# Hymba decode step: queries and keys transposed in float32, two heads at once, and split into high and low parts as they leave PSUM

## The chip, the cores and the metric

The kernel runs on one core of one Trainium2 chip. The metric is the device time of one execution in microseconds (us), as the median of several. One profiled execution of the same kernel gives the trace that the rows below come from.

## The reference

One layer of a hybrid decoder handles a prompt of 512 tokens and 8 sample tokens. After RMSNorm and one input projection, one half of the channels goes through a state-space scan and a gated unit, the other half through attention with 8 query heads of 64 values and 2 key heads. An output projection joins both. The part that matters here are the scores of two of the three attention branches of the prompt:

```python
q = rope(rms_norm(q.reshape(B, S, N_HEADS, HEAD_DIM), q_norm_w), pos)
ks = rms_norm(kv[:, :, 0::2], k_norm_w[:, None, :])
ks = rope(ks...)
...
s = jnp.einsum('bqgrd,bqgkjd->bqgrkj', q, kg, preferred_element_type=f32) * scale   # selected blocks
s = jnp.einsum('bqgrd,bwgd->bqgrw', q, kw, preferred_element_type=f32) * scale      # window
```

The scores are wanted in float32. TensorE multiplies float32r operands, so the kernel keeps each query and key as a high part (the value rounded to float32r) and a low part (the value minus the high part) and adds the products.

## The kernel before

The program is written with a tile framework. It allocates buffers from pools, adds all semaphore waits, and a scheduler with a timeline of its own decides in which order the instructions of an engine stand. `S` is ScalarE (ACT in the profile), `V` VectorE (DVE), `T` TensorE (PE), `G` GpSimd (POOL). A copy or a subtraction goes through the wrapper `PsumFirst`, so it has line L61 where it touches PSUM and L62 where it does not.

The span has three stages. From 0 to about 178 us the dense stage `dense` projects the inputs (lines L121 to L123 are the three matmuls of a product of split operands) and runs the scan. At the end the output projection `wo_mm` does the same kind of matmul. Between them `merge` interleaves two streams of steps:

- `prompt`: four `qk_tile(i)`, one for each 128 tokens, then `attention(i)`, then `glu`. `qk_tile` makes the transposed queries `QT` and keys `KT` (head dimension on the partitions, tokens along the row). For the queries of one head, partitions 0 to 63 of `QT` hold the high part and 64 to 127 the low part. For the keys of one group, `KT[g][0]` holds the high part twice, in both halves of the partitions, and `KT[g][1]` the low part twice. `attention(i)` starts with L1159 (queries against compressed keys) and L1216 (queries against keys). L1230 is the first transpose of its probabilities.
- `sample`: `compress_prompt` (L1097, L1109, then L1119, 64 small matmuls of `W1r` against `XP`, then the bias `hb` and a gelu in the tiles `gx` and `hidp`), then for each pair of sample tokens `gather_pair`: GpSimd fetches cache pages with an indirect DMA into `kvg` (L1319), VectorE copies them into `xr`, TensorE transposes them (L1328, L1338) into tiles `t`, and L1362 multiplies. The first fetches reuse the buffers of `W1r`, so they wait until L1119 has read them.

`qk_tile` before the change works in this order for a tile. ScalarE rounds 512 query columns to float32r (`qs`), VectorE subtracts to get the low part, and both stand side by side for each head. The same is done for the keys (`ks`). Then TensorE transposes with the float32r identity `identr`: L995 four times for each group of four heads, L1002 four times for the keys of a group. That is 16 transposes for a tile, 64 in all. ScalarE copies each finished bank into `QT` or `KT` in two instructions of 128 by 256.

The finished transposes land in PSUM tiles of the tag `a`, which has three banks that `attention` and the matmuls of other stages share: `BANKS = dict(a=3, t=2, c=2, ph=1)`. A bank can be written again only when its readers are done.

Of the kernel before, what the change touches and what calls it, by code (L numbers as in the profile page):

```python
# [8 lines left out]
F32 = mybir.dt.float32  # L9
F32R = mybir.dt.float32r  # L10
# [3 lines left out]
ALU = mybir.AluOpType  # L14
# [22 lines left out]
def hymba_step_kernel(  # L37
# [9 lines left out]
    G, T = nc.gpsimd, nc.tensor  # L47
# [18 lines left out]
    V, S = PsumFirst(nc.vector), PsumFirst(nc.scalar)  # L66
# [7 lines left out]
    last = {}  # L74
# [8 lines left out]
    def pt_(name, cols=1024, dt=F32, parts=128):  # L83
        return big.tile([parts, cols], dt, tag="P", name=nm(name), bufs=NP)
# [7 lines left out]
    def st(shape, name, dt=F32, bufs=1, tag=None):  # L92
        n = nm(name)
        return sm.tile(shape, dt, tag=tag or n, name=n, bufs=bufs)
# [15 lines left out]
    def pb(use):  # L110
        tag = ROUTE[use]
        return psum.tile([128, 512], F32, tag=tag, name=nm(tag), bufs=BANKS[tag])
# [48 lines left out]
    ident = cst[:, C_ID:C_ID + 128]  # L161
# [35 lines left out]
    p = pb("tr")  # L197
# [129 lines left out]
    x = lambda j, b, k: lambda: x_split(j, b, k)  # L327
# [97 lines left out]
    identb = st([128, 128], "identb", BF16)  # L425
    with tc.issue_after(last["x"].ins):
        V.tensor_copy(identb, ident)
    identr = st([128, 128], "identr", F32R)
    with tc.issue_after(last["x"].ins):
        V.tensor_copy(identr, ident)  # L430
    causb = st([128, 128], "causb", BF16)
    with tc.issue_after(last["x"].ins):
        V.tensor_copy(causb, cst[:, C_CAUS:C_CAUS + 128])
# [10 lines left out]
    def rowset(i):  # L444
        if i < 4:
            return 128, kvt[i], qraw[i // 2][:, 512 * (i % 2):512 * (i % 2) + 512]
        return 8, kvs, qsr
# [53 lines left out]
    p = pb("ac")  # L501
# [123 lines left out]
    for src, ct_ in ((c_re, CTr), (c_im, CTi)):  # L625
        cn = k2("cn", 256).rearrange("p (q n) -> p q n", n=64)
        nc.sync.dma_start(cn, src[0].rearrange("(q g) c n -> (g c) q n", q=4))
        p = pb("ac")
# [18 lines left out]
    for a, src in enumerate((state_re, state_im)):  # L647
        n0 = k1("n0")
        nc.sync.dma_start(n0, src[0].rearrange("b (a c) n -> (b a) (c n)", c=2))
        p = pb("ac")  # L650
# [312 lines left out]
    p = pb("tr")  # L963
# [12 lines left out]
    QT = [[ht("QT", 1024, F32R) for _ in range(2)] for _ in range(2)]  # L976
# [2 lines left out]
    KTv = lambda g, a: KT[g][a].rearrange("p (k n) -> p k n", k=2)  # L979

    def qk_tile(i):
        _, kv_, q_ = rowset(i)
        qs = pt_("qs", 1024, F32R).rearrange("p (h a d) -> p h a d", a=2, d=64)
        qh = q_.rearrange("p (h d) -> p h d", d=64)
        S.copy(qs[:, :, 0, :], qh)
        V.tensor_tensor(qs[:, :, 1, :], qh, qs[:, :, 0, :].bitcast(F32), op=ALU.subtract)
        ks = pt_("ks", 1024, F32R).rearrange("p (k g a e d) -> p k g a e d", k=2, g=2, a=2, d=64)
        for kd in range(2):
            kz = kv_[:, 256 * kd + 256:256 * kd + 384].rearrange("p (g d) -> p g d", g=2).unsqueeze(2).to_broadcast([128, 2, 2, 64])
            S.copy(ks[:, kd, :, 0], kz)  # L990
            V.tensor_tensor(ks[:, kd, :, 1], kz, ks[:, kd, :, 0].bitcast(F32), op=ALU.subtract)
        for g in range(2):
            p = pb("qk")
            for r in range(4):
                T.transpose(p[:, 128 * r:128 * r + 128].bitcast(F32R), qs[:, 4 * g + r].rearrange("p a d -> p (a d)"), identr)  # L995
            for hf in range(2):
                S.copy(QT[g][hf].rearrange("p (h n) -> p h n", n=512)[:, :, 128 * i:128 * i + 128],
                       p[:, 256 * hf:256 * hf + 256].rearrange("p (h n) -> p h n", n=128))
            p = pb("qk")
            for kd in range(2):  # L1000
                for a in range(2):
                    T.transpose(p[:, 256 * a + 128 * kd:256 * a + 128 * kd + 128].bitcast(F32R),  # L1002
                                ks[:, kd, g, a].rearrange("p e d -> p (e d)"), identr)
            for a in range(2):
                S.copy(KTv(g, a)[:, :, 128 * i:128 * i + 128],
                              p[:, 256 * a:256 * a + 256].rearrange("p (k n) -> p k n", n=128))
            yield 1


# [737 lines left out]
```

## Time and profile before

| what | value |
|---|---|
| median of 3 executions | 468.6 us (466.94 to 468.63) |
| the profiled execution, its own time | 465.36 us |
| its span in the profile | 463.5 us |
| granted TensorE clock, mean | 0.996 |

The time of an execution is the span and what lies around it, 1.9 us here. The profiled execution is 3.2 us below the median. How to read the rows: a row of a timeline has the start within the span, the duration of the row, and in brackets the idle time of its engine ahead of it and what ended that time. A matmul row's duration contains a pipeline of about a quarter of a microsecond, so the cost of one in a run is read from the distance of starts or from the chain, which counts each stretch of time once.

### The profile page before, as it was taken

The numbers are of one execution on the slowest core, as the hardware profiler recorded it, in microseconds if no ns is written. First come the engines' busy times: TensorE is split into PE (matmuls) and PEld (weight loads), VectorE is DVE, ScalarE is ACT, GpSimd is POOL, SyncE is SP. The second block draws the span as 40 slices with busy tenths as digits, with TensorE's granted clock in tenths as the row PEclk, the third lists the DMA queues.
The fourth block names the chain that finished last, engine by engine and source line by source line (L and its number), as shares of the span: only waits on it lengthen the run. The fifth ranks groups of instructions, "written<-read, shape, count | busy, mean of one in ns | idle before, by whom it ended". The sixth has DMA issues, their size and how long they took to land.

```text
span 463.5 us, 10940 instructions
## 1 busy us (share of the span) xinstructions
PE 449.1 (97%) x4258; PEld 382.8 (83%) x4258; DVE 348.4 (75%) x940; ACT 240.9 (52%) x585; POOL 94.7 (20%) x104
## 2 busy tenths in 40 slices
PE   8999999999999998699999999999999899999997
PEld 4989999899999998698677776767667689799886
DVE  6878999998998999385767857787658678683332
ACT  5913664756414319575765668565665646342100
POOL 3100000056433000552342224321323010000000
PEclk9999999999999999999999999999999999999999
DMA  8877533614617433566153443346354994411211
GB/s 290 251 224 174 82 72 109 187 34 90 144 50 217 137 75 75 189 184 182 45 173 100 140 180 101 128 133 232 95 175 144 229 233 144 124 58 58 69 47 48
DMA packets 75602, 62.83 MB, mean 136 GB/s; under 512 B 29230, under 2 KB 69024, under 8 KB 75424
## 3 DMA queue, kind: packets, MB, share of 16 engines
q1 hardware_dynamic: 66176, 36.74, 28.9%
q0 software_dynamic: 4816, 17.03, 11.4%
q10 hardware_dynamic: 4560, 8.39, 5.9%
q8 instruction: 33, 0.54, 0.5%
q14 instruction: 17, 0.14, 0.1%
HBM read 55.63 MB, written 10.70 MB: 143 GB/s over the span
## 4 chain that ended last, share of the span: by engine, by line
PE 71%; DVE 14%; DMA 8%; POOL 3%; issue 2%; ACT 2%; SPq 0%; DVEq 0%; POOLq 0%; ACTq 0%
PE a L121 11%; PE a L122 11%; PE a L123 10%; PE ph L1362 8%; DMA kvg<-in_cache_kv_dram,idx 4%; PE a L1216 3%; PE a L1252 3%; PE t L1243 3%; POOL rsq L168 3%; PE c L1535 3%; PE t L1338 2%; DVE ga L62 2%; PE t L1328 2%; PE ph L473 1%; DMA x<-in_x_prompt_dram 1%
## 5 line engine op out<-in xcount | busy, mean ns | idle before, releaser
L121 PE MATMUL a<-hTh,whi 128*128 128x256 f32 (+1 forms) x192 | 54.6, 285 | 0.5 <-DVE sg L61 0.5
L122 PE MATMUL a<-hTh,wlo 128*128 128x256 f32 (+1 forms) x192 | 54.9, 287 | 0.0
L123 PE MATMUL a<-hTl,whi 128*128 128x256 f32 (+1 forms) x192 | 53.4, 284 | 0.0
L168 POOL TENSOR_TENSOR rsq<-rsq,mhalf 128x6 f32<-128x6 f32 (+3 forms) x10 | 28.7, 2871 | 101.2 <-DVE rsq L62 101.2
L1319 POOL DMA_INDIRECT kvg<-in_cache_kv_dram,idx x32 | 32.6, 1020 | 67.9 <-DVE ks L62 37.7
L122 PE MATMUL a<-whi,hTl 128*128 128x256 f32 (+1 forms) x160 | 45.7, 287 | 0.0
L121 PE MATMUL a<-whi,hTh 128*128 128x256 f32 (+1 forms) x160 | 45.2, 287 | 0.0
L123 PE MATMUL a<-wlo,hTh 128*128 128x256 f32 (+1 forms) x160 | 45.2, 284 | 0.0
L1362 PE MATMUL ph<-XT,W1h 128*128 128x256 f32 x256 | 44.9, 299 | 0.2 <-ACT XT L61 0.2
L61 ACT ACTIVATE P<-a,mx 128x128 f32<-128x128 f32 (+3 forms) x64 | 33.6, 534 | 13.6 <-DVE mx L61 12.4
L61 DVE TENSOR_REDUCE mx<-a 128x1 f32<-128x384 f32 (+3 forms) x48 | 28.0, 596 | 13.1 <-PE a L1217 12.8
L121 PEld LDWEIGHTS a<-hTh,whi 128*128 128x128 f32 x192 | 36.1, 188 | 0.9 <-DVE sg L61 0.7
L122 PEld LDWEIGHTS a<-hTh,wlo 128*128 128x128 f32 x192 | 36.1, 188 | 0.9 <-DVE wlo L62 0.4
L123 PE MATMUL a<-wol,mixh 128*128 128x256 f32 x128 | 36.2, 284 | 0.0
L121 PE MATMUL a<-woh,mixh 128*128 128x256 f32 x128 | 36.1, 284 | 0.0
L1362 PEld LDWEIGHTS ph<-XT,W1h 128*128 128x128 f32 x256 | 35.0, 191 | 1.0 <-ACT XT L61 0.6
L122 PE MATMUL a<-woh,mixl 128*128 128x256 f32 x128 | 35.8, 281 | 0.0
L123 PEld LDWEIGHTS a<-hTl,whi 128*128 128x128 f32 x192 | 35.7, 188 | 0.1
L62 ACT CAST whi<-w 128x1024 fp32r<-128x1024 f32 (+4 forms) x26 | 23.9, 927 | 15.9 <-PE a L122 10.6
L122 PEld LDWEIGHTS a<-whi,hTl 128*128 128x128 f32 x160 | 30.1, 188 | 1.2 <-issue 0.9
L121 PEld LDWEIGHTS a<-whi,hTh 128*128 128x128 f32 x160 | 29.8, 188 | 0.9 <-PE ph L473 0.4
L123 PEld LDWEIGHTS a<-wlo,hTh 128*128 128x128 f32 x160 | 30.2, 189 | 0.2 <-issue 0.2
(410 smaller groups left out, 1219.4 us busy)
## 6 DMA issues: line engine op xcount, KB each, us to landing
w<-in_w_in_dram SPq DMA_DIRECT2D x16, 512.0 KB
out_dram<-in_cache_win_dram ACTq DMA_DIRECT2D x8, 511.0 KB
x<-in_x_prompt_dram SPq DMA_DIRECT2D x4, 512.0 KB
TT<-scr_k SPq DMA_DIRECT2D x4, 512.0 KB
w<-in_w_in_dram SPq DMA_DIRECT2D x16, 128.0 KB
W1r<-in_cmp_w_dram SPq DMA_DIRECT2D x4, 512.0 KB
wk<-in_cache_win_dram SPq DMA_DIRECT2D x8, 256.0 KB
wv<-in_cache_win_dram SPq DMA_DIRECT2D x8, 256.0 KB
```

Source lines behind the costliest of these rows:

```text
L61: return f(*args, **kw)
L62: return f(*args, **kw)
L121: T.matmul(out, ah, bh, start=start, stop=False, skip_group_check=True)
L122: T.matmul(out, al, bh, start=False, stop=False, skip_group_check=True)
L123: T.matmul(out, ah, bl, start=False, stop=stop, skip_group_check=True)
L168: return G.tensor_tensor(out, out, mhalf[:parts, :cols], op=ALU.pow)
L1216: T.matmul(bank, QTv(g, r)[:, qsl], KTv(g, a)[:, brs, :n], start=(a == 0), stop=False, skip_group_check=True)
L1243: T.transpose(p[:, 128 * r:128 * r + 128], P[r][:, br, 128 * kt:128 * kt + 128], ident)
L1252: mm = T.matmul(po[64 * br:64 * br + 64, :], kvt[kt - 1][:, c0:c0 + 64], behind[kt - 1][br][0], start=(kt == 1), stop=(kt == i + 1), tile_ ...
L1319: G.indirect_dma_start(out=gt_, out_offset=None, in_=ckv, in_offset=bass.IndirectOffsetOnAxis(ap=idx[:, 2 * pr_ + b2, jq:jq + 1], axis=0))
L1362: T.matmul(ph3[:, kd], (W1l if part == 1 else W1h)[kd][a][:, wsl], (xl if part == 2 else xh)[:, e, a:a + 256], start=(jq == 0 and kd == 0 ...
L1535: T.matmul(pO[32 * q:32 * q + 32, 0:128], todo[q][j][0], todo[q][j][1], start=(j == 0), stop=(j == len(todo[q]) - 1), skip_group_check=Tru ...
```

## The change

The identity in float32r is dropped. ScalarE now copies the keys twice side by side in float32 (`ks`), and the queries are transposed straight from their rows. One transpose of 128 by 128 with the float32 identity turns two heads at once, one on partitions 0 to 63 and one on 64 to 127. So a group of four heads needs two transposes and the keys of a group need two: 8 for a tile, 32 in all. The split is made on the way out of PSUM: for each head ScalarE copies 64 by 128 values to `QT` as float32r, and VectorE subtracts that copy from the same PSUM values and writes the low part. For the keys it is one copy and one subtraction of 128 by 256 for each group.

```diff
--- before.py
+++ after.py
@@ -425,9 +425,6 @@
     identb = st([128, 128], "identb", BF16)
     with tc.issue_after(last["x"].ins):
         V.tensor_copy(identb, ident)
-    identr = st([128, 128], "identr", F32R)
-    with tc.issue_after(last["x"].ins):
-        V.tensor_copy(identr, ident)
     causb = st([128, 128], "causb", BF16)
     with tc.issue_after(last["x"].ins):
         V.tensor_copy(causb, cst[:, C_CAUS:C_CAUS + 128])
@@ -979,31 +976,30 @@
     KTv = lambda g, a: KT[g][a].rearrange("p (k n) -> p k n", k=2)
 
     def qk_tile(i):
+
         _, kv_, q_ = rowset(i)
-        qs = pt_("qs", 1024, F32R).rearrange("p (h a d) -> p h a d", a=2, d=64)
-        qh = q_.rearrange("p (h d) -> p h d", d=64)
-        S.copy(qs[:, :, 0, :], qh)
-        V.tensor_tensor(qs[:, :, 1, :], qh, qs[:, :, 0, :].bitcast(F32), op=ALU.subtract)
-        ks = pt_("ks", 1024, F32R).rearrange("p (k g a e d) -> p k g a e d", k=2, g=2, a=2, d=64)
+        isl = slice(128 * i, 128 * i + 128)
+        ks = pt_("ks", 512).rearrange("p (k g e d) -> p k g e d", k=2, g=2, d=64)
         for kd in range(2):
-            kz = kv_[:, 256 * kd + 256:256 * kd + 384].rearrange("p (g d) -> p g d", g=2).unsqueeze(2).to_broadcast([128, 2, 2, 64])
-            S.copy(ks[:, kd, :, 0], kz)
-            V.tensor_tensor(ks[:, kd, :, 1], kz, ks[:, kd, :, 0].bitcast(F32), op=ALU.subtract)
+            S.copy(ks[:, kd], kv_[:, 256 * kd + 256:256 * kd + 384].rearrange("p (g d) -> p g d", g=2).unsqueeze(2)
+                   .to_broadcast([128, 2, 2, 64]))
         for g in range(2):
+
             p = pb("qk")
-            for r in range(4):
-                T.transpose(p[:, 128 * r:128 * r + 128].bitcast(F32R), qs[:, 4 * g + r].rearrange("p a d -> p (a d)"), identr)
-            for hf in range(2):
-                S.copy(QT[g][hf].rearrange("p (h n) -> p h n", n=512)[:, :, 128 * i:128 * i + 128],
-                       p[:, 256 * hf:256 * hf + 256].rearrange("p (h n) -> p h n", n=128))
+            for h in range(2):
+                T.transpose(p[:, 128 * h:128 * h + 128], q_[:, 256 * g + 128 * h:256 * g + 128 * h + 128], ident)
+            for h in range(2):
+                for e in range(2):
+                    src = p[64 * e:64 * e + 64, 128 * h:128 * h + 128]
+                    out = QTv(g, 2 * h + e)[:, isl]
+                    S.copy(out[0:64], src)
+                    V.tensor_tensor(out[64:128], src, out[0:64].bitcast(F32), op=ALU.subtract)
             p = pb("qk")
             for kd in range(2):
-                for a in range(2):
-                    T.transpose(p[:, 256 * a + 128 * kd:256 * a + 128 * kd + 128].bitcast(F32R),
-                                ks[:, kd, g, a].rearrange("p e d -> p (e d)"), identr)
-            for a in range(2):
-                S.copy(KTv(g, a)[:, :, 128 * i:128 * i + 128],
-                              p[:, 256 * a:256 * a + 256].rearrange("p (k n) -> p k n", n=128))
+                T.transpose(p[:, 128 * kd:128 * kd + 128], ks[:, kd, g].rearrange("p e d -> p (e d)"), ident)
+            p3 = p[:, 0:256].rearrange("p (k n) -> p k n", n=128)
+            S.copy(KTv(g, 0)[:, :, isl], p3)
+            V.tensor_tensor(KTv(g, 1)[:, :, isl], p3, KTv(g, 0)[:, :, isl].bitcast(F32), op=ALU.subtract)
             yield 1
 
 
```

The new lines move the code: before's L782, L787, L995, L1002, L1109, L1119, L1328 and L1362 are L779, L784, L990, L999, L1105, L1115, L1324 and L1358 after the change, and the other lines move by 3 or 4 alike. In rows of the built program a name's number tells buffers apart.

**TensorE, between the last matmuls of the scan and those of `compress_prompt`.** `t` tiles are for the states (L810, L811) and sample queries (L967), `ch` is the input of `compress_prompt`. Before:

```order
L995 MATMUL a_2893<-identr_303,qs_2885 128x128 x4
L1002 MATMUL a_2900<-identr_303,ks_2888 128x128
L995 MATMUL a_2939<-identr_303,qs_2885 128x128 x4
L1002 MATMUL a_2900<-identr_303,ks_2888 128x128 x3
L810 MATMUL t_2504<-cst_70,hfin_486 16x128
L811 MATMUL t_2504<-cst_70,hs_485 128x128
L810 MATMUL t_2504<-cst_70,hfin_486 16x128
L811 MATMUL t_2504<-cst_70,hs_485 128x128
L967 MATMUL t_2728<-cst_70,qsv_2729 128x8 x4
L969 MATMUL t_2728<-cst_70,kvs 128x8 x2
L1002 MATMUL a_2946<-identr_303,ks_2888 128x128 x4
L995 MATMUL a_2993<-identr_303,qs_2985 128x128 x4
```

and now:

```order
L122 MATMUL a_2671<-hTh_111,wlo_2461 128x264
L123 MATMUL a_2671<-hTl_115,whi_2460 128x264
L990 MATMUL a_2886<-cst_70,qraw_312 128x128 x2
L999 MATMUL a_2897<-cst_70,ks_2883 128x128 x2
L807 MATMUL t_2502<-cst_70,hfin_484 16x128
L808 MATMUL t_2502<-cst_70,hs_483 128x128
L807 MATMUL t_2502<-cst_70,hfin_484 16x128
L808 MATMUL t_2502<-cst_70,hs_483 128x128
L964 MATMUL t_2726<-cst_70,qsv_2727 128x8 x4
L966 MATMUL t_2726<-cst_70,kvs 128x8 x2
L990 MATMUL a_2934<-cst_70,qraw_312 128x128 x2
L1272 MATMUL c_2760<-KN_2725,QB_2723 32x2 x8
```

Twelve rows before hold 20 transposes for queries and keys and have not come to L1109 yet; now there are six transposes on the way to it, and two matmuls of the dense stage stand just ahead.

**VectorE, where the first cache pages come in.** `xr` copies pages that an indirect DMA brings, `hb` is the bias after L1119, `gx` the gelu behind it. Before:

```order
L62 TENSOR_TENSOR ks_3139<-kvt_312,ks_3139 128x2x128 x2
L61 TENSOR_TENSOR hb_2755<-c_2852,spT_320 128x2
L62 COPY xr_3017<-kvg_3014 128x2x4x64
L62 COPY xr_3024<-kvg_3021 128x2x4x64
L61 COPY kT_3028<-t_3013 128x512
L62 TENSOR_SCALAR gx_2956<-gx_2956 128x128
L62 TENSOR_TENSOR gx_2956<-gx_2956,gx_2955 128x128
```

and now:

```order
L61 TENSOR_TENSOR KT_2745<-a_2897,KT_2744 128x2x128
L61 TENSOR_TENSOR QT_2742<-a_2934,QT_2742 64x128
L61 TENSOR_TENSOR QT_2741<-a_2886,QT_2741 64x128
L61 TENSOR_TENSOR QT_2742<-a_2934,QT_2742 64x128
L61 TENSOR_TENSOR QT_2743<-a_2934,QT_2743 64x128 x2
L62 COPY xr_3011<-kvg_3008 128x2x4x64
L62 COPY xr_3018<-kvg_3015 128x2x4x64
L61 TENSOR_TENSOR hb_2753<-c_2850,spT_318 128x2
L61 TENSOR_TENSOR KT_2747<-a_2945,KT_2746 128x2x128
L62 TENSOR_SCALAR gx_2953<-gx_2953 128x128
L61 TENSOR_TENSOR QT_2740<-a_2985,QT_2740 64x128
L62 TENSOR_TENSOR gx_2953<-gx_2953,gx_2952 128x128
```

The subtractions of `QT` and `KT` have come into the row, and `hb` stands now behind the two copies `xr`.

**ScalarE, the first tile's copies, with the semaphores that each waits for.** `a_2886` and `a_2934` are the banks of the queries of the two groups, `a_2897` that of the keys of the first. Before:

```order
L62 CAST qs_2985<-qraw_314 128x8x64
L61 CAST QT_2742<-a_2893 128x2x128 [waits PE_49]
L61 CAST QT_2743<-a_2893 128x2x128
L62 CAST ks_2988<-kvt_310 128x2x128 [waits DVE_49,PE_49]
L62 CAST ks_2988<-kvt_310 128x2x128
```

and now:

```order
L61 CAST QT_2740<-a_2886 64x128 [waits DVE_49]
L61 CAST QT_2741<-a_2886 64x128 [waits DVE_49]
L61 CAST KT_2744<-a_2897 128x2x128 [waits PE_49]
L62 COPY ks_3131<-kvt_310 128x256 [waits DMAHW3_49,DMAHW4_49,DMAHW2_49,PE_49]
L62 COPY ks_3131<-kvt_310 128x256
L61 CAST QT_2742<-a_2934 64x128
L61 CAST QT_2741<-a_2886 64x128 [waits DVE_49]
L61 CAST QT_2742<-a_2934 64x128 [waits DVE_49]
L61 CAST QT_2743<-a_2934 64x128 [waits DVE_49] x2
```

Where two copies of 128 by 256 emptied a bank one after the other, there are now four of 64 by 128, and all but the first of a bank wait for VectorE, that is, for the subtraction of the copy before them.

## Rows read from the trace of the kernel before

**Rows 1.** The page, part 1: each engine's busy time, share of the span, instructions.
```profile
PE 449.1 (97%) x4258; PEld 382.8 (83%) x4258; DVE 348.4 (75%) x940; ACT 240.9 (52%) x585; POOL 94.7 (20%) x104
```

**Rows 2.** Windows: each stretch (us), its length, busy us of PE, PEld, DVE, ACT, POOL, clock, DMA.
```profile
178.10:192.97 14.87, 11.91 (x220) 10.99 (x220) 8.58 (x36) 10.66 (x38) 3.93 (x4) 1.00 0.36 100
192.97:214.74 21.77, 21.00 (x190) 19.25 (x191) 16.96 (x38) 14.16 (x44) 10.33 (x14) 0.92 0.66 204
...
400.00:410.00 10.00, 10.00 (x85) 8.29 (x85) 5.85 (x18) 4.38 (x10) 0.00 (x0) 1.00 0.30 94
```

**Rows 3.** Chain in time order, 165 to 235 us: start us, us, what ran or was waited for.
```profile
182.85 0.47 PE a L995 x4
183.31 0.90 PE c L1109 x8
...
189.39 5.47 DMA kvg<-in_cache_kv_dram,idx
...
230.88 4.33 DMA kvg<-in_cache_kv_dram,idx
```

**Rows 4.** PE timeline: start us, us, engine, line, operation, tiles, count [idle before <-releaser].
```profile
178.10 0.53 PE L995 MATMUL a<-identr,qs 128*128 128x128 f32 x4 [1.11 <-DVE qs L62]
...
184.79 1.15 PE L1119 MATMUL c<-XP,W1r 128*64 128x65 f32 x32
...
186.09 3.02 PE L1119 MATMUL c<-XP,W1r 128*64 128x65 f32 x96
...
192.97 0.44 PE L1328 MATMUL t<-cst,kvg 128*128 128x128 f32 x2 [2.80 <-DMA kvg<-in_cache_kv_dram,idx]
...
196.37 0.81 PE L1002 MATMUL a<-identr,ks 128*128 128x128 f32 x4
...
203.61 1.08 PE L1159 MATMUL a<-kcT,QT 128*128 128x64 f32 x8
...
214.67 0.44 PE L1230 MATMUL t<-cst,pcs 128*128 128x128 f32 x2
```

**Rows 5.** DVE timeline around the first gathered cache pages.
```profile
189.15 0.16 DVE L61 TENSOR_TENSOR hb<-c,spT 128x2 f32<-128x2 f32 x1 [1.70 <-PE c L1119]
192.95 0.43 DVE L62 COPY xr<-kvg 128x512 f32<-128x512 f32 x1 [3.63 <-DMA kvg<-in_cache_kv_dram,idx]
194.88 0.43 DVE L62 COPY xr<-kvg 128x512 f32<-128x512 f32 x1 [1.51 <-DMA kvg<-in_cache_kv_dram,idx]
```

**Rows 6.** VectorE groups, 150 to 260 us: shapes and count | busy us, mean ns of one | idle.
```profile
L62 DVE TENSOR_TENSOR ks<-kvt,ks 128x256 fp32r<-128x256 f32 x8 | 3.0, 416 | 0.0
...
L62 DVE TENSOR_TENSOR qs<-qraw,qs 128x512 fp32r<-128x512 f32 x4 | 2.7, 680 | 0.0
...
L61 DVE TENSOR_TENSOR sg<-a,rsT 128x256 f32<-128x256 f32 x4 | 1.6, 409 | 0.0
...
L62 DVE TENSOR_TENSOR hs<-hs,h 128x128 f32<-128x128 f32 x2 | 0.5, 273 | 0.0
...
L61 DVE TENSOR_TENSOR grow<-c,cst 64x96 f32<-64x96 f32 x1 | 0.2, 250 | 0.0
```

**Rows 7.** ScalarE groups, 150 to 260 us, in the same form.
```profile
L61 ACT CAST KT<-a 128x256 fp32r<-128x256 f32 x16 | 5.4, 403 | 2.7 <-PE a L1002 2.7
L61 ACT CAST QT<-a 128x256 fp32r<-128x256 f32 x16 | 5.3, 396 | 3.4 <-PE a L995 3.4
...
L62 ACT CAST ks<-kvt 128x256 fp32r<-128x256 f32 x8 | 2.9, 415 | 0.0
...
L61 ACT COPY ktt<-t 128x128 f32<-128x128 f32 x1 | 0.3, 265 | 0.1
```

**Rows 8.** Timelines of ACT and DVE: one copy out of PSUM, and its subtraction.
```profile
217.93 0.59 ACT L61 CAST XT<-t 128x512 fp32r<-128x512 f32 x1
...
218.55 0.69 DVE L61 TENSOR_TENSOR XT<-t,XT 128x512 fp32r<-128x512 f32 x1 [3.12 <-ACT XT L61]
```

## The prediction

> **What bounds the kernel now.** I read the page's busy shares first, then windows by stage, then the chain in time order, and last the timelines of TensorE and VectorE where the change lies. TensorE is busy 449.1 us, 97% of the span, VectorE 75%, ScalarE 52% [rows 1]. A share says nothing about one stage, so the windows come next. In a stretch far behind the change TensorE is busy 10.00 of 10 us [rows 2]: there it is the bound, and whatever the change does earlier only shifts it. TensorE falls short just where the queries and keys are transposed. In the 14.87 us from 178.10 to 192.97 it works 11.91, and in the 21.77 us from there to 214.74 it works 21.00 [rows 2]. In that second stretch VectorE is already busy 16.96 us, 78%. The chain names what ends the idle time: TensorE itself, then the fetch of the first cache pages (5.47 us), which cannot start before L1119 has read `W1r`, and later another fetch, 4.33 us at 230.88 [rows 3]. The timeline of TensorE has the same holes: 1.11 us for VectorE's `qs` at 178.10, and 2.80 us for the pages at 192.97 [rows 4].
>
> So the place has two parts with different limits: a front, up to the end of L1119 at 189.11 [rows 4], and the stretch from the first pages to the first L1230, which starts at 214.67 [rows 4]. In the built program the instructions stand again as before from about that L1230 to the end. I cost the two parts one by one and carry the sum through.
>
> **The change part by part.**
>
> *TensorE.* Four L995 take 0.47 us and eight float32 transposes of the same 128 by 128 shape (L1109) take 0.90 [rows 3]: 0.117 and 0.113 each. So 64 become 32 at the same price: 7.5 us become 3.6, 3.9 less. By the Trainium skill (FP8 and Floating Point Precision, TensorE Precision Notes) true float32 goes through the TensorE array in four passes. By it, 32 transposes at four times 0.117 would be an estimated 15.0 us, 7.5 more than now. The trace does not agree for transposes: the float32 ones of L1109 cost the same as L995, so the sum goes by the rows.
>
> *VectorE.* Leaving: 4 `qs` subtractions of 0.680 and 8 of `ks` at 0.416 [rows 6], 6.05 us. Coming: 32 subtractions of 64 by 128 and 8 of 128 by 256. The trace has none of 64 by 128 with two operands. The nearest rows are `grow` from PSUM, 64 by 96, at 250 ns, and `hs`, 128 by 128, at 273 ns; I take 273, which has the same row length. The 128 by 256 subtraction out of PSUM (`sg`) is 409 ns [rows 6]. Together 32 x 0.273 + 8 x 0.409 = 12.0 us. VectorE gains 6.0 us of work, because a subtraction of a quarter of a bank costs far more than a quarter of one over a whole row.
>
> *ScalarE.* Leaving: 32 copies into `QT` and `KT` at 396 and 403 ns and 8 `ks` at 415 [rows 7], and 4 `qs` at about 0.59 (the 128 by 512 copy of [rows 8]): 18.4 us. Coming: 32 copies at about 0.265 (`ktt`, 128 by 128, is the nearest), 8 at 0.403, 8 at 0.415 [rows 7]: 15.0. ScalarE gets 3.4 us lighter, and it was not the bound: 14.16 busy of 21.77 [rows 2]. I count it as nothing; the cover is its own idle time. The `identr` conversion goes too; it lies in the dense stage, far ahead of the first use, and I count it as nothing.
>
> *The front.* On TensorE 36 transposes stood ahead of L1119, now six do. By TensorE alone the front would shrink by 30 x 0.117 = 3.5 us and by the wait of 1.11 [rows 4] for `qs`, which is gone: 4.6. But L1119 also waits for the `XP` copies on VectorE. Ahead of the last of those, VectorE loses three `qs` and four `ks` subtractions (2.04 + 1.66) and takes up three of the new ones (0.82): 2.9 us less. VectorE's is the smaller, so I take **-2.9**; the ends are -2.2, if the new subtractions each wait for their copy there (another 0.23, half a copy, each), and -4.6. The first fetch is issued when L1119 ends, and so moves up as much.
>
> *From the first pages to L1230.* The first L1159 of `attention(0)` needs all its `QT` and `kcT`, and all 16 banks of queries and keys go through the three buffers `a` ahead of it. In the built order 8 query subtractions and one of keys stand ahead of the first `xr`; 24 and 7 stand behind it. So VectorE's work in the stretch grows from 16.96 by 24 x 0.273 (6.55) and 7 x 0.409 (2.86) to 26.4 us. That is more than the 21.77 that the stretch takes now, and TensorE's 21.00 there gets smaller, by 20 transposes' difference. VectorE becomes the bound of this stretch.
>
> Some idle time stays on top. `hb` now stands behind both `xr` copies. Between them VectorE waits 1.51 us for the second fetch [rows 5]. It used to have finished `hb` at 189.15, 3.6 us ahead of the first. Behind `hb` wait ScalarE's `gx`, and behind that on ScalarE its next copy of keys, whose subtraction is VectorE's next instruction: two activations and a copy, about 1.0 us by the copies of [rows 7]. So 26.4 + 1.5 + 1.0 = 28.9. Also queued behind `hb` are the copies that free the banks `a`, so TensorE cannot go on with L990 and L999 in that time; it has the `xr` transposes and then waits. This makes the stretch 28.9 - 21.8 = **+7.1**. The ends: with no idle time at all and the query subtractions at 0.200 (half of the 0.409 for twice the row) it would be 16.96 + 24 x 0.200 + 2.86 = 24.6, +2.8; with the 4.8 us of idle that VectorE has there now [rows 2] kept whole, 31.2, +9.4.
>
> There is a second cost of the same kind. A copy and a subtraction of one bank now alternate, each waiting for the other engine; the order shows the semaphore of VectorE on all but the first copy of a bank. Such a hand-off is short: a copy ends at 218.52 and its subtraction starts at 218.55 [rows 8], 0.03 us. The bank is thus held for four copies and four subtractions in a row, 4 x (0.265 + 0.273) = 2.2 us, where it was two copies, 0.8. With three banks that is 0.7 us a bank, less than VectorE's own work for the pair of banks, and so it decides only where both engines wait for each other. By the Trainium skill (PSUM — Partial Sum Buffer, PSUM bank collisions raise a hardware error) two engines may not touch one bank in the same 32-partition quadrant at once, while other quadrants are free. The two heads lie on different quadrants, so by that rule both could be emptied at once, and a bank be held an estimated 1.1 us. No row here shows two engines in one bank, and the program's semaphores keep them apart by whole banks; the sum keeps 2.2.
>
> *The rest.* From L1230 the order is the old one and TensorE is full. The waits for fetches there (4.33 us [rows 3]) follow steps that shift with it, so they stay. Sum: -2.9 + 7.1 = **+4.2**. The profiled execution took 465.36; it would take 469.6. It lies 3.2 under the median of 468.6, so against the median the forecast is **472.8 us**.
>
> **The rivals.**
>
> *It gets faster.* If VectorE keeps up, the stretch stays TensorE's, the saved transposes and the gone wait arrive, and the time falls by up to 3.9 + 1.1 = 5.0, to 463.6. It decides on the stretch from the first L1328 to L1230: at 24.7 us (21.8 + 2.9) the change breaks even, under it it wins. That asks for 31 subtractions at no more than 0.25 us with no idle time on VectorE. For it: the stretch need not end all its VectorE work before L1230 (the `sg` products could slide behind). Against it: 78% busy already, and `hb` waits by order.
>
> *No change.* VectorE is packed without idle time: 26.4 - 21.8 - 2.9 = +1.7, 470.3, or with the cheaper subtractions of 24.6 about nothing, 468.5. Against it is the 1.5 us wait for the second fetch, which stands in the order.
>
> *Much slower.* All idle time stays, and the hand-offs come on top: +9.4 - 2.9 = +6.5, or with the front's weaker end +7.2, 475.8; another couple of microseconds if a bank is held longer than 2.2.
>
> *It doesn't do what it says.* The scheduler also shifts the dense stage by a few instructions (a subtraction of `W1l` moves behind `KN`); that could cost or give some 1.1 us, the length of the wait that is gone, either way.
>
> **How the numbers follow.** Slower by VectorE (the forecast and the stronger rival): 0.66, since the work that comes is counted from the order and only its price is bounded. No change within 0.5% (2.3 us, about what a measurement here can tell): 0.20. Faster: 0.14, for what can slide behind L1230. The range leaves out most of the faster case and the very slow end: from 467.5, a little under the packed case's lower end, to 477.5, the strong rival with a longer hold of the banks. The slower cases alone would be 471 to 477.5.
>
> **What would show it.** Right, if in the profile after L1119 ends near 186.2 (189.11 now) and the first L1328 starts near 190; TensorE has waits at L990 or L999 ended by VectorE or ScalarE between there and the first L1159; VectorE is busy 90% in that stretch; L1230 starts near 219 (214.67 now); and all later rows are shifted alike. The 64 by 128 subtraction should read 0.25 to 0.30 us. Wrong in the price if it reads under 0.2; wrong in the mechanism if VectorE has idle time there and TensorE none, or if L1230 is late but the end is not, for then the wait is swallowed later, most likely in the fetch at 230.88.

## The result, and the profile after

The changed kernel takes **474.15 us** (median of 6, 472.11 to 477.27), the kernel before on the same chip 469.32 (466.94 to 471.74). The ratio is 1.010, 95% interval 1.0065 to 1.0135: about 4.8 us slower. The forecast was 472.8, in a range from 467.5 to 477.5.

The profiled execution took 473.24 with a span of 471.2, at a mean granted clock of 0.985; the one before had 463.5 at 0.996. So the two traces lie 7.7 us apart, more than the medians. Of the 102 executions of the kernel before that ran beside the experiments, 98 lie between 464.45 and 471.79 us at a clock of 0.978 to 0.996, on a line of 2.8 us for each 0.01 of mean clock; the four slower ones count in no ratio. The 0.011 between the traces is worth an estimated 3.1 us by this line, which leaves 4.6. At an equal clock, 0.983 to 0.987, the medians are 473.6 for the changed kernel (4 executions) and 469.5 for the one before (24): 4.1 us apart. So the clock of the executions doesn't explain the loss. The trace before is one of the fastest executions of its kernel, and a stretch of the two traces must be compared with this in mind.

The busy shares on the page hardly move; the line answers to [rows 1]:

```profile
PE 451.7 (96%) x4226; PEld 382.5 (81%) x4226; DVE 354.7 (75%) x967; ACT 240.1 (51%) x589; POOL 95.3 (20%) x104
```

The windows by stage answer to [rows 2]: the front ahead of L1115 (before: L1119), L1115 itself, three pieces of the stretch from the first pages on, and that stretch as a whole up to the first L1226 (before: L1230).

```profile
178.10:183.82 5.72, 3.58 (x45) 2.63 (x43) 5.14 (x24) 3.11 (x12) 0.00 (x0) 0.98 0.33 62
183.82:189.24 5.42, 5.42 (x129) 5.35 (x130) 2.71 (x9) 1.07 (x5) 1.09 (x1) 0.70 0.05 15
...
192.99:199.47 6.48, 3.50 (x13) 1.70 (x13) 3.51 (x11) 2.71 (x11) 4.21 (x6) 0.57 0.74 242
199.47:204.19 4.72, 4.72 (x36) 4.10 (x37) 4.53 (x11) 4.28 (x13) 0.00 (x0) 0.51 0.47 158
204.19:217.62 13.43, 13.14 (x115) 12.11 (x113) 11.90 (x32) 8.01 (x25) 3.98 (x6) 1.00 0.52 159
192.99:223.48 30.49, 26.49 (x201) 21.90 (x202) 25.16 (x66) 18.83 (x64) 10.23 (x14) 0.83 0.49 149
```

The stretch takes 30.49 us where it took 21.77. VectorE's work in it went from 16.96 to 25.16. TensorE is idle for 4.0 us of it (30.49 - 26.49), against 0.8 before, and the clock is 0.83 against 0.92: it runs at about half, the lower level of 1.2 GHz, up to 204. From 204 to 217.6 TensorE is full (13.14 of 13.43) and VectorE busy 11.90. Over the whole span TensorE is idle for 19.5 us (471.2 - 451.7), where it was 14.4 (463.5 - 449.1), and it is busy 2.6 us longer although it has 32 transposes less.

TensorE's timeline, in the form of [rows 4], shows where it waits:

```profile
179.46 0.44 PE L990 MATMUL a<-cst,qraw 128*128 128x128 f32 x2 [0.54 <-ACT sgS L61]
...
181.55 0.24 PE L1093 MATMUL c<-cst,pen 32*128 32x32 f32 x1 [0.65 <-DVE snew L61]
...
183.82 5.42 PE L1115 MATMUL c<-XP,W1r 128*64 128x65 f32 x128 [0.93 <-DVE XP L61]
...
192.99 0.44 PE L1324 MATMUL t<-cst,kvg 128*128 128x128 f32 x2 [2.94 <-DMA kvg<-in_cache_kv_dram,idx]
...
195.38 0.69 PE L1324 MATMUL t<-cst,kvg 128*128 128x128 f32 x2 [1.61 <-DMA kvg<-in_cache_kv_dram,idx]
...
197.31 0.69 PE L990 MATMUL a<-cst,qraw 128*128 128x128 f32 x2 [0.56 <-DVE KT L61]
198.42 0.69 PE L999 MATMUL a<-cst,ks 128*128 128x128 f32 x2 [0.42 <-DVE KT L61]
...
217.62 1.08 PE L1155 MATMUL a<-kcT,QT 128*128 128x64 f32 x8 [0.29 <-DVE QT L61]
...
221.70 0.51 PE L1212 MATMUL a<-KT,QT 128*128 128x256 f32 x2 [0.31 <-DVE QT L61]
...
223.48 0.38 PE L1226 MATMUL t<-cst,pcs 128*128 128x128 f32 x2
```

L1115 starts 1.0 us sooner than L1119 did, but takes 5.42 us where [rows 4] had 184.79 to 189.11, 4.3. The first pages land when they did (192.99 against 192.97). Of TensorE's 4.0 idle us behind them, 1.6 go to the second pages and 1.6 to the four waits shown for `KT` and `QT` subtractions; the other 0.8 wait for other work of VectorE. The first L1155 comes 14 us later than the first L1159 did (203.61). The first L1226 is 8.8 us late, but the span is only 7.7 longer. TensorE's groups in the stretch, before and then after, say what TensorE did meanwhile:

```profile
L1362 PE MATMUL ph<-XT,W1h 128*128 128x256 f32 x48 | 8.5, 300 | 0.0
L1362 PE MATMUL ph<-XT,W1l 128*128 128x256 f32 x24 | 4.1, 285 | 0.0
L995 PE MATMUL a<-identr,qs 128*128 128x128 f32 x8 | 1.4, 306 | 0.0
L1002 PE MATMUL a<-identr,ks 128*128 128x128 f32 x8 | 1.4, 306 | 0.0
```

```profile
L1358 PE MATMUL ph<-XT,W1h 128*128 128x256 f32 x52 | 10.1, 320 | 0.0
L1358 PE MATMUL ph<-XT,W1l 128*128 128x256 f32 x28 | 4.9, 300 | 0.0
L999 PE MATMUL a<-cst,ks 128*128 128x128 f32 x10 | 2.2, 308 | 0.4 <-DVE KT L61 0.4
L990 PE MATMUL a<-cst,qraw 128*128 128x128 f32 x10 | 2.2, 307 | 0.6 <-DVE KT L61 0.6
```

Eight more products of the sample stream (80 for 72) stand ahead of the first L1226, about 1.0 us of work that is then missing behind it, and four more transposes (20 for 16). The windows from there to the end, before and after, agree:

```profile
214.74:463.50 248.76, 241.62 (x2032) 191.89 (x2031) 158.97 (x399) 126.53 (x304) 45.99 (x63) 1.00 0.42 128
```

```profile
223.48:471.20 247.72, 240.63 (x2025) 190.97 (x2023) 159.09 (x403) 127.85 (x312) 45.42 (x63) 1.00 0.42 128
```

TensorE is idle for 7.1 us there both times and has 1.0 us less to do. The clock is 1.00 in both, so the lower mean clock of the trace after was lost further ahead, in the front and the stretch that the change touches.

The new instructions in VectorE's, ScalarE's and TensorE's groups, 150 to 260 us, in the form of [rows 6, 7]:

```profile
L61 DVE TENSOR_TENSOR QT<-a,QT 64x128 fp32r<-64x128 f32 x32 | 9.0, 288 | 2.1 <-ACT QT L61 1.2
L61 ACT CAST QT<-a 64x128 fp32r<-64x128 f32 x32 | 8.2, 261 | 10.0 <-DVE QT L61 9.3 <-PE a L990 0.5
...
L61 DVE TENSOR_TENSOR KT<-a,KT 128x256 fp32r<-128x256 f32 x8 | 3.4, 422 | 1.2 <-ACT KT L61 1.1
L61 ACT CAST KT<-a 128x256 fp32r<-128x256 f32 x8 | 3.0, 370 | 0.2 <-PE a L999 0.2
```

One price of TensorE comes from the chain, for two transposes:

```profile
177.58 0.22 PE a L990 x2
```

### The profile page after: what moved, and what is told of

It reads as the page before. It is cut to its first block, busy times and chain, and to the rows that moved or that the text cites. A ratio compares the mean times of both kernels' runs of the same rounds, so it can differ in the third digit from the quotient of the medians.

```text
span 471.2 us, 10892 instructions
## 1 busy us (share of the span) xinstructions
PE 451.7 (96%) x4226; PEld 382.5 (81%) x4226; DVE 354.7 (75%) x967; ACT 240.1 (51%) x589; POOL 95.3 (20%) x104
## 4 chain that ended last, share of the span: by engine, by line
PE 70%; DVE 11%; DMA 6%; POOL 5%; issue 4%; ACT 3%; SPq 0%; POOLq 0%; ACTq 0%; DVEq 0%
PE a L121 11%; PE a L122 11%; PE a L123 11%; PE ph L1358 8%; PE a L1212 3%; POOL rsq L168 3%; DMA kvg<-in_cache_kv_dram,idx 3%; PE a L1248 3%; PE t L1239 3%; PE c L1531 2%; PE t L1334 2%; PE t L784 1%; PE t L1324 1%; DVE wlo L62 1%; DVE ga L62 1%
## 5 line engine op out<-in xcount | busy, mean ns | idle before, releaser
L168 POOL TENSOR_TENSOR rsq<-rsq,mhalf 128x6 f32<-128x6 f32 (+3 forms) x10 | 29.9, 2998 | 100.8 <-DVE rsq L62 100.8
L1358 PE MATMUL ph<-XT,W1h 128*128 128x256 f32 x256 | 45.8, 303 | 0.2 <-ACT XT L61 0.2
L1358 PEld LDWEIGHTS ph<-XT,W1h 128*128 128x128 f32 x256 | 35.6, 194 | 1.4 <-ACT XT L61 0.6
L62 ACT CAST whi<-w 128x1024 fp32r<-128x1024 f32 (+4 forms) x26 | 23.8, 925 | 15.4 <-PE a L122 15.3
```

Of the source, the lines that this page charges most:

```text
L62: return f(*args, **kw)
L168: return G.tensor_tensor(out, out, mhalf[:parts, :cols], op=ALU.pow)
L1358: T.matmul(ph3[:, kd], (W1l if part == 1 else W1h)[kd][a][:, wsl], (xl if part == 2 else xh)[:, e, a:a + 256], start=(jq == 0 and kd == 0 ...
```

## The experiments

Four theories were held against each other. Theory 2, which the prediction rests on: VectorE's added work binds the stretch. Against it: the bias `hb` stuck behind the second fetch (theory 1), the alternation of two engines on a bank, and TensorE's granted clock (theory 3). All results together; each ratio is to the kernel before, run beside it.

| run | what | median us | before | ratio (95% interval) |
|---|---|---|---|---|
| changed kernel | | 474.15 | 469.32 | 1.0100 (1.0065 to 1.0135) |
| e1 | `hb` ahead of `xr` | 473.62 | 468.40 | 1.0109 (1.0071 to 1.0148) |
| e2 | copies ahead of subtractions | 472.34 | 468.40 | 1.0078 (1.0048 to 1.0107) |
| e3 | 64 by 256, half as many | 471.34 | 468.40 | 1.0066 (1.0038 to 1.0094) |
| e4 | each transpose twice | 477.02 | 468.40 | 1.0176 (1.0135 to 1.0217) |
| e5 | no low part of the queries | 467.28 | 469.06 | 0.9983 (0.9952 to 1.0014) |
| e6 | low part of two columns | 471.19 | 469.06 | 1.0061 (1.0028 to 1.0094) |
| e7 | keys alone | 467.59 | 469.06 | 0.9996 (0.9962 to 1.0030) |
| e8 | queries alone | 471.08 | 469.06 | 1.0079 (1.0054 to 1.0105) |
| e9 | changed, TensorE's holes filled | 472.37 | 469.33 | 1.0079 (1.0050 to 1.0107) |
| e10 | keys alone, holes filled | 470.29 | 469.33 | 1.0034 (1.0004 to 1.0064) |
| e11 | e6 and e2 | 468.86 | 468.67 | 1.0008 (0.9979 to 1.0037) |
| e12 | e3, e2 and e1 | 469.44 | 468.67 | 1.0014 (0.9987 to 1.0041) |

An interval is about 0.3% to each side, 1.4 us. Neighbours in the table can't be told apart; e5, e7, e11 and e12 against the changed kernel can.

**e1.** `hb` ahead of the `xr` copies on VectorE:

```diff
+        last["hb"] = V.tensor_tensor(hb, ph[:, 64:130:65], b1T, op=ALU.add)
...
+                with tc.issue_after(last["hb"].ins):
+                    V.tensor_copy(xr_...)
```

> The bias hb is put ahead of the two xr copies on VectorE; nothing else moves. Theory 1 (hb stuck behind the second fetch holds ScalarE's copies and with them the banks): hb runs at about 189.4 instead of 195.8, ScalarE's idle time of 9.06 us shrinks to about 3, the copies and subtractions of two more banks are done before the first pages land, and the end comes 2 to 4 us sooner than the changed kernel's 474.2, so 470 to 472. Theory 2 (VectorE's 31 added subtractions bind the stretch, wherever they stand): only what moves into the wait for the pages counts, about 2 x 0.42 + 2 x 0.28 = 1.4 us: 472.8. Theory 3 (TensorE's lower clock after its idle time is the loss): the clock between 193 and 204 stays near 0.55 and the gain is under 1 us.

The ratio is that of the changed kernel. The timelines show why. First VectorE in the changed kernel, `hb` right behind the second `xr`, and the first subtraction of `KT` 1.0 us after it, and ScalarE's wait for `hb`:

```profile
192.97 0.43 DVE L62 COPY xr<-kvg 128x512 f32<-128x512 f32 x1 [5.69 <-DMA kvg<-in_cache_kv_dram,idx]
195.36 0.43 DVE L62 COPY xr<-kvg 128x512 f32<-128x512 f32 x1 [1.97 <-DMA kvg<-in_cache_kv_dram,idx]
195.82 0.16 DVE L61 TENSOR_TENSOR hb<-c,spT 128x2 f32<-128x2 f32 x1
196.83 0.42 DVE L61 TENSOR_TENSOR KT<-a,KT 128x256 fp32r<-128x256 f32 x1 [0.85 <-ACT KT L61]
...
196.01 0.52 ACT L61 ACTIVATE gx<-c,hb 128x64 f32<-128x64 f32 x2 [9.06 <-DVE hb L61]
```

then VectorE in e1, where `hb` runs 3.9 us ahead of the first `xr`:

```profile
190.57 0.16 DVE L61 TENSOR_TENSOR hb<-c,spT 128x2 f32<-128x2 f32 x1 [2.11 <-PE c L1115]
194.47 0.43 DVE L62 COPY xr<-kvg 128x512 f32<-128x512 f32 x1 [3.74 <-DMA kvg<-in_cache_kv_dram,idx]
196.51 0.43 DVE L62 COPY xr<-kvg 128x512 f32<-128x512 f32 x1 [1.61 <-DMA kvg<-in_cache_kv_dram,idx]
196.85 0.42 DVE L61 TENSOR_TENSOR KT<-a,KT 128x256 fp32r<-128x256 f32 x1
```

and ScalarE in e1, the first copy after the second pages:

```profile
197.75 0.26 ACT L61 CAST QT<-a 64x128 fp32r<-64x128 f32 x1 [5.59 <-DVE QT L61]
```

`hb` comes 5 us sooner and ScalarE goes on, but VectorE's own next instructions are still the two `xr`, and the subtractions stand behind them; in the changed kernel VectorE waits 5.69 us for the first pages with 31 subtractions in its queue behind them. ScalarE now waits 5.59 us for a subtraction instead of 9.06 for `hb`. Theory 1 named a real wait with the wrong owner: what counts is where VectorE's subtractions stand. In the trace the stretch is 1.1 us shorter (194.46 to 223.80), which the times don't show. Theory 3 had expected a gain under 1 us too, at a clock near 0.55 from 193 to 204, and it read 0.60; so e1 speaks against theory 1 alone.

**e2 and e3.** All copies of a bank ahead of its subtractions; and `QT` laid out so that one instruction takes two heads:

```diff
+            for lo in range(2):
                 for h in range(2):
                     for e in range(2):
...
+                        if lo == 0:
+                            S.copy(out[0:64], src)
+                        else:
+                            V.tensor_tensor(out[64:128], src, out[0:64].bitcast(F32), op=ALU.subtract)
```

```diff
+    QTv = lambda g, r: QT[g][r % 2][:, 512 * (r // 2):512 * (r // 2) + 512]
...
+            for e in range(2):
+                src = p[64 * e:64 * e + 64, 0:256].rearrange("p (h n) -> p h n", n=128)
+                out = QT[g][e].rearrange("p (h n) -> p h n", n=512)[:, :, isl]
```

> All four copies of a bank of queries are issued ahead of its four subtractions, so that a bank changes hands once and not seven times; the same instructions with the same sizes, in another order. Theory 2 (VectorE's added work binds): the work is the same 12.0 us, so the gain is what finds room ahead of the first pages, at most 2 to 3 us, and the kernel stays slower than the one before (over 470). Rival (the alternation of the two engines on a bank, and the order that the scheduler makes of it, is the loss): most transposes and subtractions move ahead of the first pages, the first L1155 comes 8 us or more sooner than 217.6, and the time falls to the kernel before or under it, 465 to 469.

> QT is laid out so that the two heads of the same half of the partitions lie in one tile: a bank is emptied by two copies and two subtractions of 64 by 256 instead of four and four of 64 by 128; copy and subtraction still alternate. Theory 2 (VectorE's work): 32 x 0.28 becomes 16 x 0.41, 2.4 us less, and the time falls by about that, to 471.8. Rival (alternation and order): three hand-offs a bank instead of seven, half of the loss goes, 468 to 470. If a subtraction of 64 by 256 costs twice the one of 64 by 128, nothing changes.

The group of copies in e2:

```profile
L61 ACT CAST QT<-a 64x128 fp32r<-64x128 f32 x32 | 8.4, 261 | 4.8 <-PE a L990 4.5
```

and the group of subtractions in e3:

```profile
L61 DVE TENSOR_TENSOR QT<-a,QT 64x256 fp32r<-64x256 f32 x16 | 6.8, 423 | 0.5
```

In e2 ScalarE's copies wait for TensorE alone, not for VectorE (9.3 us in the changed kernel). The scheduler now puts many subtractions ahead of the `XP` copies, so that L1118 (L1115 of the changed kernel) starts only at 187.7. The first L1158 (L1155 there) comes at 212.5, 5 us sooner, where the rival asked for 8. The gain is 1 to 2 us, in the range that theory 2 gave, and the rival's 465 to 469 did not come. In e3, 2.2 us less on VectorE (9.0 to 6.8) bring 1.6 to 2.8 us, by ratio or by median, as theory 2 had it; but e3 also has fewer hand-offs, and neither gain is clear of the intervals.

**e4.** `for _ in range(2):` ahead of each new transpose.

> Each of the 32 new transposes is done twice into the same place, so TensorE has again 64 of them, as before the change; everything else is the same but for what the scheduler moves. By TensorE's work alone it is 3.6 us slower than the changed kernel where TensorE is the bound and 0 where it waits: 474 to 478. Theory 3 (TensorE's clock falls because the transposes that filled its idle time are gone): the clock in the stretches from 183 to 204 rises again towards 1.00 in the front and 0.74 behind it, L1115 takes about 4.3 us instead of 5.4, and the time is the same or lower, 471 to 474.

477.0 lies in the 474 to 478 that TensorE's work alone gives: doubled, the 3.6 us of transposes cost 2.9 by medians and 3.6 by ratio. In this stretch TensorE isn't idle enough to hide them. As a test of the clock it failed, for the clock did not rise (0.73 from 184 to 189, 0.55 and 0.60 behind the pages): the doubled transposes stand behind the same waits as the single ones.

**e5 and e6.** The 32 subtractions left out, and the same on two columns of 128; the rest of the low part is zeros, written once by GpSimd:

```diff
-                    V.tensor_tensor(out[64:128], src, out[0:64].bitcast(F32), op=ALU.subtract)
```

```diff
+                    V.tensor_tensor(out[64:128, 0:2], src[:, 0:2], out[0:64, 0:2].bitcast(F32), op=ALU.subtract)
```

> The 32 subtractions of 64 by 128 are left out and the low parts of the queries are zeros, written once ahead; transposes, copies and keys as changed. Theory 2 (VectorE's added work binds the stretch): 32 x 0.28 = 9 us less for VectorE, the first L1226 comes back to about 214 to 216, and the time to 466 to 468, the kernel before or a little under it. Theory 3 (TensorE's clock falls because it has fewer transposes to fill its idle time): the transposes stay at 32, the clock stays near 0.55 from 193 to 204 and the time stays above 471.

> The 32 subtractions stay in their places with their waits, but each works on two of 128 columns (the other low parts are zeros): the alternation of the two engines on a bank stays, and nearly all of the work goes. If the length of VectorE's work is the loss (theory 2): the time comes near that of the run without the subtractions, within 1.5 us, 466 to 469. If the hand-offs themselves are the loss: it stays at 471 to 474.

e5 gives it all back: 0.9983, and the first transpose of the probabilities at 218.2 instead of 223.5 (214 to 216 was expected), though its pages came 2.4 us later. Its trace has the clock of the changed kernel's, 0.984, so it speaks against theory 3 as the main cause. Its page:

```profile
PE 450.8 (97%) x4226; PEld 384.1 (82%) x4226; DVE 346.5 (74%) x935; ACT 241.0 (52%) x589; POOL 99.6 (21%) x108
```

With a span of 465.9 TensorE is idle for 15.1 us, 4.4 less than in the changed kernel, of 5.3 by which the spans differ. Fewer transposes with the same copies do no harm; the subtractions, with the waits that come with them, do. That is the plainest result of the study. But e6, at 471.19, lies in the range given to the hand-offs; it kept more than expected, and its group of subtractions says part of it:

```profile
L61 DVE TENSOR_TENSOR QT<-a,QT 64x2 fp32r<-64x2 f32 x32 | 4.9, 158 | 2.7 <-ACT QT L61 1.9
```

A subtraction of 2 columns takes 158 ns, one of 128 takes 288. So e6 kept 4.9 of the 9.0 us, and could not tell length from hand-off as it was meant to.

**e7 and e8.** One half of the change alone, by putting the old lines of `ks` and L1002, or of `qs` and L995, back:

> Only the keys are done in the new way (16 float32 transposes, split on the way out, 8 subtractions of 128 by 256 as before); the queries in the old way. TensorE has 16 transposes less than the kernel before, 1.9 us, ScalarE 8 copies less, VectorE the same 6.05 us. Theory 2: no loss, 466.5 to 468.5. Theory 3: less to fill TensorE's idle time, lower clock, 469 to 471.

> Only the queries are done in the new way; the keys are split ahead of their transposes as before the change. Theory 2: all of the added work of VectorE is in the queries (8.7 in place of 2.7 us), so nearly the whole loss stays, 472 to 475. If the keys or their subtraction behind hb are the loss, 468 to 470.

The keys alone cost nothing (0.9996), the queries alone nearly all (1.0079), as theory 2 said; the median of 471.08 lies under the 472 that was expected. The keys keep 8 subtractions of the same size, the queries go from 4 to 32. But e7 did not gain the 1.9 us of TensorE either. Windows of its front, in the columns of [rows 2]:

```profile
176.00:184.00 8.00, 6.65 (x72) 5.54 (x70) 6.11 (x17) 5.54 (x18) 0.00 (x0) 0.71 0.44 93
184.00:189.00 5.00, 5.00 (x29) 4.28 (x30) 3.10 (x17) 3.97 (x13) 0.00 (x0) 0.50 0.06 18
```

The clock fell to its half there, and L1117 ended at 193.2, 4 us later than before. That led to e9 and e10.

**e9 and e10.** Transposes of the identity into a bank that nobody reads, in TensorE's holes:

```diff
+    fz = pb("ph")
+    def fill(n, after):
+        for _ in range(n):
+            with tc.issue_after(after.ins):
+                after = T.transpose(fz[:, 0:128], ident, ident)
...
+        fill(20, mw)
```

> The changed kernel with 37 transposes of the identity added, into a bank that nobody reads: 4, 5, 4 and 4 where TensorE had idle time ahead of L1115, 20 behind L1115 in the wait for the pages. They should cost TensorE nothing (17 x 0.11 = 1.9 us into 2.1 us of holes, 20 x 0.11 = 2.2 into 2.9). Theory 3 (the granted clock, which fell to 0.70 in L1115 and 0.57 behind the pages): the clock stays near 1.00 up to 193, L1115 takes 4.1 us, all that follows comes 1 to 2 us sooner, and the time is 472 to 473.3. Theory 2 alone: no gain beyond that, so still over 470; if the whole loss was the clock, 469.

> Only the keys in the new way, and 40 transposes of the identity in the same kind of holes (10 behind the scan, 3, 3, 2 and 2 ahead of L1115, 20 behind it). Run e7 had the clock at 0.71 and 0.50 from 176 to 189 and its L1115 (L1117 there) ended at 192.9, 4 us later than the kernel before. If the clock is what kept e7 at 467.6, the clock is near 1.00 there, the pages come 2 to 4 us sooner and the time is 463.5 to 466, under both kernels. If not, it stays at 467 to 468.5.

Windows of e9: L1125 (L1115 of the changed kernel), and the stretch from the first pages; then the rows of L1125:

```profile
184.80:189.10 4.30, 4.30 (x131) 4.06 (x130) 3.13 (x10) 1.54 (x6) 0.95 (x1) 1.00 0.06 19
...
193.60:223.50 29.90, 27.14 (x206) 23.20 (x207) 26.18 (x66) 18.97 (x64) 9.98 (x14) 0.83 0.51 168
```

```profile
184.79 1.15 PE L1125 MATMUL c<-XP,W1r 128*64 128x65 f32 x32
...
186.24 3.02 PE L1125 MATMUL c<-XP,W1r 128*64 128x65 f32 x96
```

The fill does what it should to the clock in the front: 1.00, and L1125 takes 4.5 us with two transposes in its middle, near the 4.3 of the kernel before. Yet the kernel gains 1.0 us by ratio, within the intervals; its 472.37 lies in the 472 to 473.3 that theory 3 gave, and far from the 469 of a loss that is all clock. The stretch behind the pages is about as long as it was, with VectorE busy 26.18 of 29.90. So the clock in the front is not the main loss. The clock behind the pages stayed at 0.83, and no run repairs it alone. e10 missed: the clock reads 1.00 from 176 to 193.5, the first pages land at 193.57 where e7 had 196.79, as hoped, and still the kernel is no faster than e7, by its median slower. Why is not settled; the intervals of the two overlap.

**e11 and e12.** The two columns with the copies first, to tell the hand-offs of e6 from its 4.9 us; and all three repairs together:

> The subtractions on two columns as in e6, with all four copies of a bank ahead of them as in e2: 32 short instructions of about 0.16 us and no alternation. If e6 kept 3.9 us over the run without subtractions because of the alternation (theory: hand-offs), this one comes to 467 to 468.5. If because 32 x 0.16 = 4.9 us of VectorE's time are left whatever their place (theory 2), it gains no more over e6 than e2 did over the changed kernel, 1.8 us: 469 to 471.5.

> The wide layout of e3, both copies of a bank ahead of both subtractions as in e2, and hb ahead of the xr copies as in e1. If these gains are of different things and add (2.8 + 1.8 + 0.5): 469, the kernel before. If all three act on the same wait of VectorE, no more than the best of them: 471. Under 467 would beat both kernels; no theory gives that.

The groups of subtractions in e2 and e11:

```profile
L61 DVE TENSOR_TENSOR QT<-a,QT 64x128 fp32r<-64x128 f32 x32 | 9.3, 289 | 0.5
```

```profile
L61 DVE TENSOR_TENSOR QT<-a,QT 64x2 fp32r<-64x2 f32 x32 | 5.0, 158 | 0.6
```

e11 takes 0.5% less than e6, 2.5 us, with the same 5 us of subtractions on VectorE. So there the alternation has a price of its own; on the full subtractions e2 had shown 1 to 2 us. With e2 it also shows the price of the length: in the same order, copies first, 4.3 us less of VectorE's work take the ratio from 1.0078 to 1.0008, 3.3 us. Under alternation the shorter work gave 1.8 us (1.0100 to 1.0061), which the intervals don't show clearly. So length and alternation both cost, and neither alone is the loss. e12 comes out level with the kernel before. By medians that is the sum of the three gains; by ratios the gains of e1 (none), e2 and e3 would leave 1.0044, so the three together gave at least their sum, and more than the best of them alone (e3, 1.0066). No version beat the kernel before: e5 leaves work out and is no faster beyond its interval.

## Why the prediction was right

The direction held, and so did its reason: VectorE's added subtractions cost the time, and without them (e5) the loss is gone. The size held by the medians, but partly by luck: two terms missed, both to the fast side, by 2.9 and 1.6 us. Of the signs that the prediction named, the length of a subtraction and the waits at L990 and L999 came. L1115 ended at 189.2 (186.2 was named), the first pages landed at 193.0 (190), VectorE was busy 83% of the stretch (90%), and the first L1226 came at 223.5 (219).

**TensorE's price** held: 0.11 us for a float32 transpose (0.22 for two), as [rows 3] gave. The Trainium skill's four passes for true float32 (FP8 and Floating Point Precision, TensorE Precision Notes) would make it an estimated 0.47; no run here shows them for transposes.

**VectorE's price** held: 0.288 us where 0.273 was taken, 0.422 where 0.409 was; 9.0 + 3.4 = 12.4 us against 12.0. It was the term that mattered: e5 removes the 9.0 and the loss is gone. e6 shows why cutting a subtraction into four is dear: of the 0.288 us, 0.158 is there with 2 columns already. ScalarE's price held too (0.261 for 0.265).

**The front, -2.9, failed.** It measured nothing: the pages landed at 192.99 instead of 192.97. L1115 did start 1.0 us sooner, not 2.9, because three waits came in that the sum had at zero: 0.54 for ScalarE, 0.65 and 0.93 for VectorE, which has the last `W1l` and three subtractions between them. The other 1.1 us went to L1115 itself, at a granted clock of 0.70 for 5.42 us. The step counted VectorE's busy time as if its chain were packed, and TensorE's clock as fixed. Its weaker end, -2.2, was mis-added too: half a copy is 0.13 by the 0.265 of [rows 7], not 0.23.

**The stretch, +7.1, was too small** in the trace: 30.49 - 21.77 = 8.7. VectorE's work was 25.16 where 26.4 was forecast: the 24 and 7 subtractions are there (24 x 0.288 + 7 x 0.422 = 9.9), and 15.3 of other work instead of 16.96. But its idle time was 5.3 and not 2.5. The wait for the second pages was 1.97 where 1.5 was priced, and the chain from `hb` to the first `KT` subtraction 1.0, as priced; the other 2.4 are many small waits, among them those between copies and subtractions. The text let the alternation decide "only where both engines wait for each other", at no cost; e2 and e11 put 1 to 2.5 us on it. The clock was missing as well, 0.83 against 0.92, in the pieces where TensorE had waited; how much of the 1.6 each of the two makes, no run separates. And VectorE is the bound of only a part of the stretch: from 199.5 to 217.6 TensorE is full, with more work than the text gave it. The text had TensorE's work get smaller by "20 transposes' difference", but 16 transposes stood behind the first pages before and 20 stand there now.

In the traces, then, 4.2 + 2.9 + 1.6 = 8.7 us are lost by L1226, and 1.1 of them are work that was only moved ahead of it. The 7.7 that stay are far from the 4.2 of the sum. By the line above an estimated 3.1 of them go with the lower mean clock, which leaves 4.6, near the 4.8 of the medians. But the trace after lost that clock in the front and the stretch, the places that were summed. Whether the kernel before loses it there too in its executions at 0.985 isn't shown, since its one trace is of 0.996. So the two misses of 4.5 us are about the size of the clock's share and of the moved work, which the sum didn't have either: that the medians came within 1.4 us of the forecast is luck in this part.

**`hb` as an own term** fell: with `hb` out of the way (e1) no gain is seen, since the subtractions wait behind the same `xr` copies.

**The rivals.** "It gets faster" asked for 31 subtractions of no more than 0.25 us on average with VectorE never idle; they took 0.32 (9.9 / 31), and 5.3 us were idle. "No change" asked for a VectorE without idle time; the changed kernel has 5.3 us of it, and e12, with less work and fewer waits, does come out level (1.0014). "Much slower", at 475.8, lies within the changed kernel's six executions, but its price for the front failed like the forecast's.

## What to carry to other kernels

An edit that halves one engine's instructions may multiply another's: count instructions on the engine that empties the banks, and price them by the shortest one in the trace, not by the element. Where two engines empty one bank, issue all of the first engine's reads and then all of the second's, and make each as wide as the layout allows: with `hb` moved as well, that took the loss of this change from 1.0% to nothing that the intervals show (e12). Work that is freed ahead of a fetch is worth only what the fetch's start moves, and that is read from the chain that ends there, not from one engine's busy time.

## What the runs showed of the hardware

Executions of one and the same program differ by their granted clock: 98 of the kernel before, from 464.45 to 471.79 us, follow the mean clock (0.978 to 0.996) at 2.8 us per 0.01. A small wait of TensorE in a place with short matmuls can be followed by several us at half clock: in e7 from 180 to 188, after 1.16 us of waiting, where the kernel before had waited 1.11 us at the same place [rows 4] and kept 1.00. The wait alone does not tell them apart. Repairing that clock with idle transposes moved the clock as wanted and the time hardly. And a VectorE subtraction out of PSUM takes 158 ns for 2 columns, 288 for 128 and 423 for 256 on 64 partitions.

The row of that wait in e7, and the window behind it:

```profile
178.61 0.54 PE L995 MATMUL a<-identr,qs 128*128 128x128 f32 x4 [1.16 <-DVE XT L62]
```

```profile
180.00:188.00 8.00, 7.81 (x59) 6.52 (x57) 5.07 (x24) 5.37 (x19) 0.00 (x0) 0.50 0.22 47
```
